# The largest expert's chunks in three parts of two weight tiles, spread over the whole-weight chunks

## The chip, the cores and the metric

The kernel runs on one core of one Trainium2 chip. The metric is the device time of one execution in microseconds (us). Before the change the median of three runs is 2092.88 us (2088.6 to 2093.2). The engines are named as the profile names them: PE (matrix multiply) with PEld (its weight loads), DVE (vector), ACT (scalar), POOL, and SP, which here only issues transfers.

## The reference

The model has two layers. Layer 0 is a mixer and a dense feed-forward network; layer 1 is a mixer and a mixture of experts (MoE). The change is in the MoE alone:

```
logits = (h @ router); top_v, top_i = top_k(logits, 2); gates = softmax(top_v)
for e in range(8):
    out += dense_gate[..., e] * ((silu(h @ w1[e]) * (h @ w3[e])) @ w2[e])
```

There are 256 tokens, `D_MODEL` = 1024 and `D_FF_EXPERT` = 3584. The weights of the eight experts, 3 x 1024 x 3584 float32 values each, are 352 MB, and every one is read once.

## The kernel before

**Experts.** After routing, the experts are put in an order `p`: `p` = 0 is expert 0, and the seven others follow by falling number of tokens. `CAPS` gives each a number of slots: 128, 192, 128, and 64 for each of the five from `p` = 3 on. So `p` = 1 is the largest expert; its 192 tokens lie in two blocks, `xs[1]` (128) and `xs[8]` (64). Tokens are gathered into slots by small matmuls (`gather_k`, L1543) and added back to their rows by others (`comb` in `finish`, L1801). These small pieces are put in a list `fills`, and `fill()` (L1667) runs one of them after each weight tile of `stage_a`.

**Chunks and weight tiles.** The 3584 hidden columns of an expert are handled in 7 chunks of 512. A chunk has six weight tiles of 128 x 2048 float32 (1 MB each): two of w1, two of w3 and two of w2. `stage_a` (L1681) multiplies tokens by the w1 and w3 tiles and forms silu x product; `stage_t` (L1730) transposes this on PE; `stage_b`, called by `stage_2` (L1845), multiplies it by the two w2 tiles. The order is skewed: within `stage_a` of a chunk (after its second tile) the transposes of the chunk before run, and behind `stage_a` comes `stage_2` of the chunk before.

**Whole and split weights.** For `p` >= 3 (`WH` = 3) a tile is used as it lies ("whole"): a float32 matmul with 64 token columns, which takes half of the array, so that two run side by side. For `p` = 0, 1, 2 each tile is split into a high and a low part by `split` (L268): ACT writes the high part from the raw tile (L269), then DVE the low part (L270), and PE multiplies high x high, low x high and high x low in its faster fp32r form (only two products for `xs[8]`, whose high and low tokens lie side by side).

**Order of the chunks.** `jobs` (L1447) holds the seven chunks of `p` = 0, then of 2, then the 35 whole chunks of `p` = 3 to 7. Behind the whole chunks number 2, 7, 12, 17, 22, 27 and 31 it holds one chunk of `p` = 1, as a job like the others. So four split tiles of `p` = 1 come in a row, then four tiles of the next whole chunk, then two more split tiles of `p` = 1.

**Buffers and lookahead.** All weight tiles, raw, high and low alike, come from one pool `w` of `NWT` = 11 buffers (L1406). `plan` lists the loads in the order of use. `prime` (L1426) first sees to it that `LEADS` (5 in this stretch) tiles are in `loaded`, which means that their DMA is issued on SP, and then moves one from `loaded` to `ready`: a whole tile as it is, a split tile by its two instructions, which need two more buffers. `next_w` (L1433) primes until two tiles are in `ready`, and hands out the first. SP issues in order: a load whose buffer isn't free yet holds up the loads behind it. ACT, DVE and PE work in order too; a scheduler of the framework fixes each engine's order when the kernel is built, with the order of the program as its priority.

**Other pools.** Token blocks lie in `xg` (4 buffers of 8 KB per partition), chunk results in `g`, transposed results in `gh` (2 buffers) and `gl`. PSUM banks for chunk results are taken in turn from tags `ax` and `pt`, two banks each.

Of the kernel before, what the change touches and what calls it, by code (L numbers as in the profile page):

```python
# [18 lines left out]
P = 128  # L19
# [148 lines left out]
def tile_backbone(ctx: ExitStack, tc: tile.TileContext, A, out, upto=99, dbg=None):  # L168
# [1278 lines left out]
    jobs = []  # L1447
    job = 0
    for p in (0, 2, 3, 4, 5, 6, 7):
        for c in range(7):  # L1450
            jobs.append((p, c))
            if p >= WH:
                if job in (1, 6, 11, 16, 21, 26, 30):
                    jobs.append((1, sum(j[0] == 1 for j in jobs)))
                job += 1
    ws = {}

    def w_get(p):
        if p not in ws:
            ws[p] = w_of(p)  # L1460
        return ws[p]

    for n in range(len(jobs) + 1):
        if n < len(jobs):
            for i in range(4):
                plan.append(lambda p=jobs[n][0], c=jobs[n][1], i=i: load2(w_get(p)[0](c, i), p >= WH))
        if n:
            for q in range(2):
                plan.append(lambda p=jobs[n - 1][0], c=jobs[n - 1][1], q=q, n=n: load2(w_get(p)[1](c, q), p >= WH,
                                                                                 2 if n == len(jobs) else 1))  # L1470

    def moe(mp, dw, oh0):
# [35 lines left out]
        def xg128():  # L1508
            return Pair(mp.tile([P, 2, KD, P], F32R, tag="xg", name="xg", bufs=4))
# [157 lines left out]
        def fill():  # L1667
            if fills:
                fills.pop(0)()
# [43 lines left out]
        def stage_t0(gd, g3):  # L1713
# [8 lines left out]
            gf = mp.tile([P, 512], F32, tag="gh", name="gf", bufs=2)  # L1722
# [3 lines left out]
            gh, gl_ = [mp.tile([P, 4, P], F32R, tag=n, name=n, bufs=2) for n in ("gh", "gl")]  # L1726
# [3 lines left out]
        def stage_t(gl):  # L1730
# [3 lines left out]
            for g, kind in gl:  # L1734
# [4 lines left out]
                if kind == 0:  # L1739
                    gf = mp.tile([P, 4, 64], F32, tag="gh", name="gf", bufs=2)  # L1740
# [3 lines left out]
                gh = mp.tile([P, 4, P], F32R, tag="gh", name="gh", bufs=2)  # L1744
# [34 lines left out]
        def closing(k):  # L1779
            if k == 0:  # L1780
                end["ss"] = bank("po")
            if not k and "x" not in end:
                end["sq"], end["x"] = [mp.tile([P, KD, 256], F32, tag="xg", name=n, bufs=4) for n in ("sq", "xf")]
                end["dg"] = hp([P, 4, P], "dg")
# [44 lines left out]
        def prep_b():  # L1829
            xs[2], xs[3] = xg128(), [mp.tile([P, KD, 64], F32, tag="xg", name="xf", bufs=4)]  # L1830
            ohTs[2], ohTs[3] = prep([spec(2), spec(3, io=iotd)], [xs[2], xs[3]], True)

        def prep_c(a):
            t = mp.tile([P, 2, KD, 64], F32, tag="xg", name="xf", bufs=4)
            xs[a], xs[a + 1] = [t[:, 0]], [t[:, 1]]
            ohTs[a], ohTs[a + 1] = prep([spec(a, io=iotd), spec(a + 1, io=iotd)], [xs[a], xs[a + 1]], True)
# [27 lines left out]

        prev = None
        gT = []
        for p, c in jobs:
# [14 lines left out]
            gl = stage_a1(*a0) if prev is None else stage_a([xs[1], xs[8]] if p == 1 else [xs[p]], mid)  # L1882
# [98 lines left out]
```

## Time and profile before

| | before |
|---|---|
| median of 3 runs | 2092.88 us |
| profiled execution, own time | 2092.78 us |
| its span (first to last instruction) | 2091.0 us |
| mean granted TensorE clock | 0.984 of full speed |
| busy: PE, PEld, DVE, ACT, POOL | 96%, 66%, 57%, 40%, 5% |
| HBM read | 493.4 MB, mean 236 GB/s over the span |
| weight tiles of the MoE, DMAs of 1 MB | 334 whole, and 2 more in halves |

The profiled execution is the median run to 0.1 us. The span is divided by the page into 40 slices of 52 us; PEclk is the clock granted to PE, DMA the mean busy share of the 16 DMA engines, GB/s what they moved. The MoE's weights move from about 1140 us on; the whole chunks, and with them all chunks of `p` = 1, begin at about 1400 us. A view by stretches gives, for each, the busy time of each engine, the granted clock, the DMA share and the rate. PE's busy time is overstated where matmuls overlap: an instruction of 0.39 us can follow the one before by 0.23 us. So work on PE is counted from start to start.

### The profile page before, as it was taken

To read this page: it belongs to the slowest core of one execution; us is meant where nothing else is said; L and a number is where in the kernel's file an instruction comes from. 1 tells how busy PE (TensorE), PEld (TensorE's weight loads), DVE (VectorE), ACT (ScalarE), POOL (GpSimd) and SP (SyncE) were. 2 spreads that over 40 slices of the span, in tenths; PEclk is the share of its full clock that TensorE was granted. 3 is DMA by queue.
4 is the path that set the end of the run, shared out by engine and by line. 5 is a ranking of instruction groups with operands and counts; after the bars stand their busy time and mean duration, and the time that the engine had idled before them with its cause. 6 is when DMAs were issued, how large, how long until landed. Compare 5 with 4: busy or idle time off the path is not lost. (4 is left out here: it accounts for less than half of the span.)

```text
span 2091.0 us, 26240 instructions
## 1 busy us (share of the span) xinstructions
PE 1999.0 (96%) x10002; PEld 1375.9 (66%) x10002; DVE 1200.4 (57%) x1842; ACT 833.3 (40%) x1261; POOL 109.9 (5%) x148
## 2 busy tenths in 40 slices
PE   7999999889999999999999999998999999899997
PEld 4776756688777878888888888855353544444453
DVE  5366557777566664765477888853253343333443
ACT  4346525643222223544356776733132222222221
POOL 0000015600000000100101000000000000000000
PEclk9999999999999999999999999999999999999998
DMA  8423432025444673322253999996999999899994
GB/s 323 149 91 97 150 121 95 27 65 161 142 150 151 211 237 127 125 61 81 82 230 134 332 364 329 319 375 246 419 368 420 392 419 397 350 398 405 396 382 171
DMA packets 89443, 496.22 MB, mean 237 GB/s; under 512 B 10080, under 2 KB 10848, under 8 KB 46048
## 3 DMA queue, kind: packets, MB, share of 16 engines
q1 hardware_dynamic: 89312, 494.49, 63.7%
q8 instruction: 81, 1.33, 0.3%
q14 instruction: 50, 0.41, 0.1%
HBM read 493.40 MB, written 1.05 MB: 236 GB/s over the span
## 5 line engine op out<-in xcount | busy, mean ns | idle before, releaser
L270 DVE TENSOR_TENSOR w<-w 128x2048 fp32r<-128x2048 f32 (+1 forms) x144 | 289.1, 2022 | 78.3 <-ACT w L269 65.8
L269 ACT ACTIVATE whi<-raw 128x1024 fp32r<-128x1024 f32 x151 | 160.0, 1060 | 406.0 <-PE bk_mm L298 264.8
L269 ACT ACTIVATE w<-w 128x2048 fp32r<-128x2048 f32 (+1 forms) x144 | 241.3, 1699 | 71.2 <-DVE w L270 23.1
L270 DVE TENSOR_TENSOR wlo<-raw,whi 128x1024 fp32r<-128x1024 f32 x151 | 186.1, 1233 | 141.5 <-ACT whi L269 139.1
L297 PE MATMUL bk_mm<-fH,whi 128*128 128x512 f32 (+1 forms) x360 | 139.9, 390 | 2.0 <-DVE xT L518 1.2
L299 PE MATMUL bk_mm<-fH,wlo 128*128 128x512 f32 (+1 forms) x360 | 138.9, 387 | 2.1 <-DVE wlo L270 2.1
L1551 PE MATMUL bk_pt<-w,xf 128*64 128x512 f32 x560 | 138.8, 600 | 1.1 <-ACT g L1704 0.6
L297 PE MATMUL bk_mm<-hH,whi 128*128 128x512 f32 (+1 forms) x384 | 137.4, 361 | 2.3 <-ACT hH L269 2.3
L298 PE MATMUL bk_mm<-fL,whi 128*128 128x512 f32 (+1 forms) x360 | 139.2, 388 | 0.0
L298 PE MATMUL bk_mm<-hL,whi 128*128 128x512 f32 (+1 forms) x384 | 136.2, 356 | 0.0
L299 PE MATMUL bk_mm<-hH,wlo 128*128 128x512 f32 (+1 forms) x384 | 135.5, 354 | 0.0
L1763 PE MATMUL bk_mm<-w,gf 128*64 128x512 f32 x560 | 132.5, 598 | 2.2 <-DMA w<-in_m 1.9
L1551 PE MATMUL bk_ax<-w,xf 128*64 128x512 f32 x560 | 132.7, 596 | 0.1
L1704 ACT COPY g<-bk_ax 64x512 f32<-64x512 f32 x42 | 24.5, 582 | 259.5 <-PE bk_ax L1551 259.3
L456 POOL TENSOR_TENSOR rstd<-rstd,mhalf 128x2 f32<-128x2 f32 (+2 forms) x11 | 10.3, 938 | 1493.3 <-DVE rstd L455 1474.2
L1551 PEld LDWEIGHTS bk_ax<-w,xf 128*64 128x64 f32 x560 | 39.2, 137 | 74.7 <-issue 69.7
L1705 DVE TENSOR_TENSOR g<-g,bk_ax 64x512 f32<-64x512 f32 x42 | 28.4, 675 | 101.3 <-ACT g L1704 101.3
L297 PEld LDWEIGHTS bk_mm<-hH,whi 128*128 128x128 f32 x384 | 71.7, 188 | 21.8 <-issue 5.4
L1763 PEld LDWEIGHTS bk_mm<-w,gf 128*64 128x64 f32 x560 | 38.1, 136 | 71.3 <-issue 68.4
L1551 PEld LDWEIGHTS bk_pt<-w,xf 128*64 128x64 f32 x560 | 38.7, 136 | 69.2 <-issue 63.4
L297 PEld LDWEIGHTS bk_mm<-fH,whi 128*128 128x128 f32 x360 | 68.1, 190 | 22.6 <-issue 3.6
L298 PEld LDWEIGHTS bk_mm<-hL,whi 128*128 128x128 f32 x384 | 72.2, 188 | 13.2 <-issue 3.4
(568 smaller groups left out, 4364.3 us busy)
## 6 DMA issues: line engine op xcount, KB each, us to landing
w<-in_m SPq DMA_DIRECT2D x334, 1024.0 KB, 9.5
raw<-in_f SPq DMA_DIRECT2D x66, 512.0 KB, 3.7
araw<-in_adc SPq DMA_DIRECT2D x56, 512.0 KB, 4.0
araw<-in_ada SPq DMA_DIRECT2D x32, 512.0 KB, 7.0
raw<-in_evx SPq DMA_DIRECT2D x29, 512.0 KB, 3.7
raw<-in_odx SPq DMA_DIRECT2D x22, 512.0 KB, 3.6
raw<-in_evo SPq DMA_DIRECT2D x12, 512.0 KB, 3.7
xT<-in_xt SPq DMA_DIRECT2D x4, 1024.0 KB, 5.5
```

The costliest lines, as they stand in the source:

```text
L269: a = S.activation(hi, src, AF.Copy)
L270: v = V.tensor_tensor(lo, src, hi.bitcast(F32), op=ALU.subtract)
L297: T.matmul(o, wh, xh, start=first, stop=False)
L298: T.matmul(o, wh, xl, start=False, stop=False)
L299: T.matmul(o, wl, xh, start=False, stop=last)
L456: G.tensor_tensor(r, r, mhalf[:, :n], op=ALU.pow)
L1551: T.matmul(o[c:c + 64], sl(b[0]), wh, start=k < 2, stop=k >= K - 2, tile_position=(0, c))
L1704: S.copy(g[0:64], hb[b][0][64:128])
L1705: V.tensor_tensor(g[0:64], g[0:64], hb[b][0][0:64], op=ALU.add)
L1763: T.matmul(accs[0][half][64 * q2:64 * q2 + 64], gT[0][0][:, f, :], wh[:, hs], start=first and q == 0, stop=last and q == 1, tile_position= ...
```

## The change

The order of work becomes a list `seq` of whole-chunk entries `(p, c, None)` and of parts `(1, c, part)`. A chunk of `p` = 1 is three parts of two split tiles each: part 0 the w1 tiles, part 1 the w3 tiles, part 2 the w2 tiles. The 21 parts are spread by the count of whole chunks; at most one stands between two whole chunks. By the formula they stand behind whole chunks 3, 5, 6, 8, 9, 11, 12, 14, 15 and so on to 32 and 33: two parts for every three whole chunks.

```diff
-    for p in (0, 2, 3, 4, 5, 6, 7):
-        for c in range(7):
-            jobs.append((p, c))
-            if p >= WH:
-                if job in (1, 6, 11, 16, 21, 26, 30):
-                    jobs.append((1, sum(j[0] == 1 for j in jobs)))
-                job += 1
+    for p in (0, 2, 3, 4, 5, 6, 7):
+        for c in range(7):
+            seq.append((p, c, None))
+            if p >= WH:
+                whole_chunks += 1
+                while parts < min(21, (whole_chunks - 1) * 21 // 32):
+                    seq.append((1, parts // 3, parts % 3))
+                    parts += 1
```

The lookahead counts `loaded` and `ready` together (six tiles), and whole tiles may be handed on ahead, up to four in `ready`, until a split tile stands in `ready`. So the two instructions of a split come up to three tiles earlier in the program:

```diff
-        while plan and len(loaded) < n:
+        while plan and (not loaded or len(loaded) + max(len(ready), 1) < n + 1):
             fetch()
...
-        while len(ready) <= AHEAD and (loaded or plan):
+        while (len(ready) <= AHEAD or len(ready) < 4 and all(w[1] is None for w in ready)) and (loaded or plan):
             prime()
```

A new function `unit` does a part. Its instructions are those that `stage_a` and `stage_2` did for `p` = 1; the result of part 0 waits in two tiles of a new tag `gb` (2 buffers) for part 1. The transposes for part 2 are done within the whole chunk ahead of it, behind that chunk's own.

```diff
+        def unit(c, part):
+            if part == 2:
+                stage_2(1, c, gTb.pop())
+                return
+            blocks = [xs[1], xs[8]]
+            hb = [bank("ax") for _ in blocks]
+            for q in range(2):
+                wh, wl = next_w()
+                for k4 in range(4):
+                    k, cs = q * 4 + k4, slice(k4 * 512, k4 * 512 + 512)
+                    for o, blk in zip(hb, blocks):
+                        mmb(o, blk, lambda x: x[:, k, :], wh[:, cs], wl[:, cs], k == 0, k == 7, k, 8)
+                fill()
...
             def mid():
-                if prev is not None:
-                    gT.append(stage_t(prev[1]))
+                gT.append(stage_t(prev[1]))
+                if n + 1 < len(seq) and seq[n + 1][2] == 2:
+                    gTb.append(stage_t(list(zip(big, (2, 1)))))
```

Besides, `xg` has 3 buffers in place of 4 (the blocks of `p` = 3 to 6 share one of them), and `gh` has 3 in place of 2.

## Rows read from the trace of the kernel before

**Rows 1.** The page's view of the span in 40 equal slices: the rate of all transfers.

```profile
GB/s 323 149 91 97 150 121 95 27 65 161 142 150 151 211 237 127 125 61 81 82 230 134 332 364 329 319 375 246 419 368 420 392 419 397 350 398 405 396 382 171
```

**Rows 2.** The view by stretches for the whole stage of the whole chunks. Columns: from:to, length, busy us (and instructions) of PE, PEld, DVE, ACT, POOL, granted clock, DMA share, GB/s.

```profile
1400.00:2060.00 660.00, 621.76 (x2756) 308.96 (x2754) 251.45 (x312) 173.22 (x211) 0.00 (x0) 0.97 0.94 382
```

**Rows 3.** The same view, the stage cut so that stretches with splits of `p` = 1 and stretches without alternate.

```profile
1400.00:1470.00 70.00, 63.98 (x274) 38.34 (x272) 28.61 (x32) 21.45 (x33) 0.00 (x0) 0.93 0.72 283
1470.00:1510.00 40.00, 38.38 (x186) 12.89 (x184) 9.65 (x16) 7.18 (x12) 0.00 (x0) 1.00 1.01 420
1510.00:1560.00 50.00, 45.69 (x198) 28.52 (x195) 24.59 (x27) 17.70 (x17) 0.00 (x0) 0.97 0.91 367
1560.00:1610.00 50.00, 47.11 (x224) 16.64 (x222) 12.67 (x21) 8.25 (x13) 0.00 (x0) 1.00 1.01 418
1610.00:1660.00 50.00, 47.02 (x192) 29.17 (x192) 21.98 (x19) 15.36 (x15) 0.00 (x0) 0.93 0.96 390
1660.00:1700.00 40.00, 38.71 (x188) 13.82 (x186) 13.13 (x24) 7.40 (x13) 0.00 (x0) 1.00 1.01 419
1700.00:1750.00 50.00, 48.33 (x210) 28.62 (x208) 23.33 (x22) 17.60 (x17) 0.00 (x0) 1.00 0.98 395
1750.00:1800.00 50.00, 45.71 (x217) 15.36 (x214) 12.65 (x22) 10.35 (x15) 0.00 (x0) 1.00 1.01 421
1800.00:1850.00 50.00, 44.67 (x182) 28.88 (x181) 21.95 (x22) 14.53 (x14) 0.00 (x0) 0.90 0.82 323
1850.00:1900.00 50.00, 46.41 (x221) 16.05 (x219) 13.33 (x22) 9.42 (x14) 0.00 (x0) 1.00 1.01 420
1900.00:1950.00 50.00, 47.42 (x195) 29.53 (x194) 21.24 (x19) 14.41 (x15) 0.00 (x0) 0.93 0.94 380
1950.00:1980.00 30.00, 30.00 (x147) 10.82 (x144) 11.20 (x21) 7.11 (x12) 0.00 (x0) 1.00 1.01 421
1980.00:2060.00 80.00, 78.33 (x350) 40.32 (x346) 37.11 (x50) 22.46 (x26) 0.00 (x0) 1.00 0.95 381
```

**Rows 4.** The same view for single places: a stretch of `p` = 0 and 2 (every tile split), the stop at the first chunk of `p` = 1, a place of two-tile splits, a place of four-tile splits, and the end of the loads.

```profile
1200.00:1250.00 50.00, 50.00 (x222) 40.31 (x221) 42.75 (x24) 34.84 (x24) 0.00 (x0) 1.00 0.99 365
...
1410.00:1430.00 20.00, 14.50 (x58) 11.13 (x58) 7.30 (x5) 9.81 (x18) 0.00 (x0) 0.74 0.17 59
...
1550.00:1560.00 10.00, 10.00 (x46) 7.07 (x45) 7.43 (x9) 2.40 (x2) 0.00 (x0) 1.00 0.67 248
...
1700.00:1730.00 30.00, 29.32 (x130) 18.21 (x128) 13.50 (x11) 11.21 (x10) 0.00 (x0) 1.00 1.01 419
...
2050.00:2060.00 10.00, 10.00 (x51) 3.60 (x50) 3.02 (x6) 0.90 (x2) 0.00 (x0) 1.00 0.81 312
2060.00:2070.00 10.00, 9.51 (x47) 3.24 (x48) 2.80 (x5) 1.47 (x3) 0.00 (x0) 1.00 0.01 2
```

**Rows 5.** Groups of instructions from 1400 to 2060 us: line, engine, operation, tiles, shapes and count, then busy us, mean ns of one, and idle time before them with what ended it.

```profile
L1763 PE MATMUL bk_mm<-w,gf 128*64 128x512 f32 x528 | 125.2, 598 | 2.2 <-DMA w<-in_m 1.9
L270 DVE TENSOR_TENSOR w<-w 128x2048 fp32r<-128x2048 f32 x42 | 95.9, 2290 | 55.3 <-ACT w L269 51.7 <-DMA w<-in_m 3.1
L269 ACT ACTIVATE w<-w 128x2048 fp32r<-128x2048 f32 x42 | 80.3, 1911 | 48.7 <-PE bk_ax L1559 23.1 <-DMA w<-in_m 20.1 <-DVE w L270 5.4
L1554 PE MATMUL bk_ax<-w,xg 128*128 128x512 f32 x56 | 25.8, 461 | 9.5 <-ACT w L269 9.5
L1555 PE MATMUL bk_ax<-w,xg 128*128 128x512 f32 x56 | 25.8, 460 | 7.3 <-DVE w L270 7.3
...
L1555 PE MATMUL bk_ax<-w,gh 128*128 128x512 f32 x28 | 11.7, 418 | 5.4 <-DVE w L270 5.4
```

**Rows 6.** PE in order of time: start, us, line, operation, tiles, count. First the combination of one result block (four matmuls, L1815 and L1816) up to the next matmul, then the 40 matmuls of the two w3 tiles of `p` = 1 up to the next whole tile, then one whole chunk from its first matmul to that of the next one.

```profile
1400.83 0.39 PE L1815 MATMUL bk_ada<-ohT,yh 128*128 128x256 f32 x1
...
1401.50 1.94 PE L1551 MATMUL bk_pt<-w,xf 128*64 128x512 f32 x8
...
1433.72 0.39 PE L1554 MATMUL bk_pt<-w,xg 128*128 128x512 f32 x1
...
1443.18 3.65 PE L1763 MATMUL bk_mm<-w,gf 128*64 128x512 f32 x16
...
1466.55 3.65 PE L1551 MATMUL bk_ax<-w,xf 128*64 128x512 f32 x16
...
1477.45 3.60 PE L1551 MATMUL bk_ax<-w,xf 128*64 128x512 f32 x16
```

**Rows 7.** The first stop. SP's longest wait between 1410 and 1430 us, then ACT in order of time at the end of the stop (evacuations of gathers, L1536, and the first split, L269), then the first matmul of `p` = 1 on PE.

```profile
SPq L1412 <- DVE w L270: 12.8, 1, 12.8
```

```profile
1419.01 0.31 ACT L1536 ACTIVATE xf<-bk_ada,mod 128x64 f32<-128x64 f32 x1 [1.31 <-PE bk_ada L1526]
1419.22 1.90 ACT L269 ACTIVATE w<-w 128x2048 fp32r<-128x2048 f32 x1
```

```profile
1421.17 0.80 PE L1554 MATMUL bk_ax<-w,xg 128*128 128x512 f32 x1 [2.20 <-ACT w L269]
```

**Rows 8.** Weight tiles issued between 1380 and 1410 us: number, size, median us from issue to landing.

```profile
w<-in_m SPq DMA_DIRECT2D x9, 1024.0 KB, 8.8
```

**Rows 9.** PE at the end: the last weight matmuls, and the first matmul of the last combination.

```profile
2066.17 5.37 PE L1763 MATMUL bk_mm<-w,gf 128*64 128x512 f32 x24
2071.53 0.38 PE L1815 MATMUL bk_ax<-ohT,yh 128*128 128x256 f32 x1
```

More of the change, by code (lines that the diff above doesn't have):

```diff
@@ L1461, in w_get, with plan_tiles @@
         return ws[p]
[L1463 to L1470, printed above, removed]
+    def plan_tiles(p, c, ins, outs, parts=1):
+        for i in ins:
+            plan.append(lambda p=p, c=c, i=i: load2(w_get(p)[0](c, i), p >= WH))
+        for q in outs:
+            plan.append(lambda p=p, c=c, q=q: load2(w_get(p)[1](c, q), p >= WH, parts))
+    last = None
+    for p, c, part in seq:
+        if part is None:
+            plan_tiles(p, c, range(4), ())
+            if last:
+                plan_tiles(*last, (), range(2))
+            last = p, c
+        elif part < 2:
+            plan_tiles(p, c, range(2 * part, 2 * part + 2), ())
+        else:
+            plan_tiles(p, c, (), range(2))
+    plan_tiles(*last, (), range(2), 2)
     def moe(mp, dw, oh0):
@@ L1743, in stage_t @@
                     continue
-                gh = mp.tile([P, 4, P], F32R, tag="gh", name="gh", bufs=2)
+                gh = mp.tile([P, 4, P], F32R, tag="gh", name="gh", bufs=3)
                 if kind == 2:
@@ L1782, in closing @@
             if not k and "x" not in end:
-                end["sq"], end["x"] = [mp.tile([P, KD, 256], F32, tag="xg", name=n, bufs=4) for n in ("sq", "xf")]
+                end["sq"], end["x"] = [mp.tile([P, KD, 256], F32, tag="xg", name=n, bufs=3) for n in ("sq", "xf")]
                 end["dg"] = hp([P, 4, P], "dg")
@@ L1829, in prep_b @@
         def prep_b():
-            xs[2], xs[3] = xg128(), [mp.tile([P, KD, 64], F32, tag="xg", name="xf", bufs=4)]
+            xs[2], t = xg128(), mp.tile([P, 4, KD, 64], F32, tag="xg", name="xf", bufs=3)
+            for i in range(4):
+                xs[3 + i] = [t[:, i]]
             ohTs[2], ohTs[3] = prep([spec(2), spec(3, io=iotd)], [xs[2], xs[3]], True)
         def prep_c(a):
-            t = mp.tile([P, 2, KD, 64], F32, tag="xg", name="xf", bufs=4)
-            xs[a], xs[a + 1] = [t[:, 0]], [t[:, 1]]
+            if a == 6:
+                xs[7] = [mp.tile([P, KD, 64], F32, tag="xg", name="xf", bufs=3)]
             ohTs[a], ohTs[a + 1] = prep([spec(a, io=iotd), spec(a + 1, io=iotd)], [xs[a], xs[a + 1]], True)
@@ L1863, in stage_2 @@
                 finish(ysp[1], 8, ohTs[8])
+        big, gTb = [], []
+        def unit(c, part):
[11 more added lines that the diff above has]
+                fill()
+            if part == 0:
+                big[:] = [mp.tile([P, 512], F32, tag="gb", name="gb", bufs=2) for _ in blocks]
+                S.activation(big[0], hb[0], AF.Silu)
+                g = big[1][0:64]
+                S.copy(g, hb[1][64:128])
+                V.tensor_tensor(g, g, hb[1][0:64], op=ALU.add)
+                S.activation(g, g, AF.Silu)
+                return
+            V.tensor_tensor(big[0], big[0], hb[0], op=ALU.mult)
+            g, g3 = big[1][0:64], mp.tile([64, 512], F32, tag="g", name="g3", bufs=3)
+            S.copy(g3, hb[1][64:128])
+            V.tensor_tensor(g3, g3, hb[1][0:64], op=ALU.add)
+            V.tensor_tensor(g, g, g3, op=ALU.mult)
         prev = None
         gT = []
-        for p, c in jobs:
+        for n, (p, c, part) in enumerate(seq):
+            if part is not None:
+                unit(c, part)
+                continue
             if (p, c) == (0, 1):
```

14 lines of the change are left out of this document (7 added, 7 removed).

## The prediction

> **What bounds the kernel now.** I read the rate by slices first [rows 1]: only from about the twenty-third slice on does the rate go to 320 GB/s and above. That is the MoE. All that the change touches lies between 1400 us, where the whole chunks begin, and the end, so I read that stage alone. It moved 0.382 x 660 = 252.1 MB in 660 us [rows 2].
>
> Next, the stage in stretches [rows 3]. The reader is to see two kinds that alternate. Where no tile is split, the DMA share is 1.01 and the rate 418 to 421 GB/s: the transfers set the pace and PE follows. Where tiles of `p` = 1 are split, the rate falls to 283, 367, 390, 395, 323, 380, 381. Against 420 GB/s this is time lost, length x (1 - rate/420): 22.8 + 6.3 + 3.6 + 3.0 + 11.5 + 4.8 + 7.4 = 59.4 us. About 2 us of the last lie behind the last landing, since the slice from 2050 has a share of 0.81 and the next 0.01 [rows 4]; so loads end at about 2058 us and the loss is 57.4 us. 22.8 us of it is at the first chunk of `p` = 1, and 34.6 us at the six others.
>
> Why it is lost: at the first chunk the DMA share is 0.17 for 20 us [rows 4]. SP waits 12.8 us for one buffer, which DVE frees by a split [rows 7]; that split stands in ACT's and DVE's order behind evacuations of gathers, and PE's first matmul of `p` = 1 waits for it until 1421 us. So PE, SP and ACT hold each other up: a row of four split tiles takes eight buffers beyond its four raw ones, of 11 in all.
>
> PE is the other limit. A whole chunk takes 1477.45 - 1466.55 = 10.9 us and two split tiles 1443.18 - 1433.72 = 9.46 us [rows 6]. From 1400 to 2060 us there are 528/16 = 33 whole chunks [rows 5], 21 pairs of split tiles and 28 combinations (four each for `p` = 2 to 6, eight for `p` = 1) at 0.67 us [rows 6]: 360 + 199 + 19 = 578 us of 660. A tile of 1.049 MB at 420 GB/s lands each 2.50 us, so a whole chunk is 15.0 us of transfers against 10.9 us of PE, and a pair of split tiles 5.0 against 9.46. Neither engine is the bound throughout; what is lost is lost because the two kinds of work come in lumps that 11 buffers can't level.
>
> **The change part by part.** Instructions: the same 1 MB loads, the same 42 splits in this stage at 1.91 us on ACT and 2.29 us on DVE [rows 5], the same matmuls, transposes, evacuations. Nothing is removed or added, only moved; the static cost is 0. The narrower pools: `xg` with 3 buffers still has each block's buffer free when it is gathered (the block of `p` = 7 takes that of `p` = 2, done before), so I cost them at nothing; were it not so, PE would wait once for one chunk, 11 us at most.
>
> The order. Two parts for three whole chunks are 18 + 4 = 22 tiles, 54.9 us of transfers, against 3 x 10.9 + 2 x 9.46 = 51.6 us of PE, and about 1.6 us for combinations (24 over 31 whole chunks). So each period is nearly level, and transfers lead by a little. How far PE falls behind within a period: a part adds 9.46 - 5.0 = 4.5 us, a whole chunk takes off 4.1. Part, whole, part gives 4.5 - 4.1 + 4.5 = 4.9 us, and the next two whole chunks take off 8.2. Before: four split tiles 8.9, minus 4.1, plus 4.5: 9.3 us. Where a split is not begun ahead, its 1.91 + 2.29 = 4.2 us come on top in both. So the lag at the worst place is about half. In buffers: (4.9 + 4.2)/2.50 = 3.6 tiles landed and not used, one in use, three for pairs, leave 3.4 of 11 for loads under way. At full rate a load took 8.8 us to land [rows 8], 8.8/2.50 = 3.5 under way. It just fits.
>
> What is left of the loss, term by term.
> - The first stop, 22.8 us: from 0 to 22.8. The first part comes one whole chunk later, with two split tiles in place of four, and four of the eight gathers done by then. I take 3.
> - The 20 other parts. Bound below 0: between 1700 and 1730 us a group of four split tiles ran at 419 GB/s [rows 4]. Bound above: 34.6 us over six chunks is 12 groups, 2.9 us for a group, if a group costs the same whatever its size; by tiles it is 34.6/36 = 0.96 us, 1.9 for a part. As the lag is half, I take half of 1.9, 0.95 us: 19 us for 20 parts.
> - The end. The last weight matmuls end at 2071.5 us [rows 9], 13.5 behind the last landing. In the new order the last group leaves 4.4 us less lag, but two whole chunks follow it in place of three (4.1 less taken off): 0, between -8 and +5.
>
> Sum: 57.4 - 3 - 19 = 35.4 us. From the profiled execution's own 2092.8 us, which is the median of the three runs to 0.1 us: **2057 us**.
>
> Does PE fit into that? Up to the new end of its weight matmuls, 2071.5 - 35.4 = 2036, it has 636 us for 578 + 10 (what it did from 2060 to 2071) + about 10 for transposes of `p` = 1: 38 us are left for waits and low clock. Its waits for splits were 9.5 + 7.3 + 5.4 = 22.2 us [rows 5]; and a granted clock of 0.93, 0.97, 0.93, 0.90, 0.93 in the mean (it goes between 2.4 and 1.2 GHz) cost it 4.9 + 1.5 + 3.5 + 5.0 + 3.5 = 18 us more [rows 3], always where it had stood still. This is close: a part may expose no more than 38/21 = 1.8 us. The cover is the early split; without it, see the second rival.
>
> Two rules speak to whether the loss can be had back at all. The whole stretches show 418 to 421 GB/s [rows 3]. The Trainium skill, page "DMA: Bandwidth & Descriptors", Specifications, gives an HBM limit of about 358 GB/s for a core; by that the 252.1 MB would take 704 us, more than they did, and no order could gain; by the rows it is 600 us, so the rows decide.
>
> The second: in rows 3 the shares alone leave 19.6 + 4.5 + 2 + 1 + 9 + 3 + 4 - 2 = 41 us idle, and 16 us of the loss is a low rate under busy DMA engines, as in 1200 to 1250 us (0.99 and 365 GB/s with DVE busy 43 of 50 us) but not in 1700 to 1730 (419, DVE 13.5 of 30) [rows 4]. If splits slow transfers, those 16 us stay, since the number of splits stays, and 41 us is the most to be gained (2052 us). The Trainium skill, page "SBUF — State Buffer", Who interferes with whom, says a DMA never contends with a compute engine; by that all 57 us could be had (2035 us). My 22 us left over lie beyond both.
>
> **The rivals.**
> - *Loss goes by tiles, not by lag.* Each part costs 1.9 us and the first 5: 57.4 - 38.6 - 5 = 14 us, 2079 us. For it: two-tile groups lost as well as four-tile ones (4.1 us in 1550 to 1560 us, 10 x (1 - 248/420)) [rows 4]. Against: there the lag of the four before them was still there.
> - *PE becomes the bound.* If each of 21 parts exposes what a group of four did, 22.2/7 = 3.2 us, because raw tiles land just when they are wanted and an early place in the order helps nothing, PE needs 598 + 67 = 665 us from 1400: 2065 in place of 2071.5, 2086 us; with the 18 us of low clock as before, 2104. The middle, 2095 us, is no change. For it: transfers lead by only 1.7 us a period, so PE often stands before a split. Against: standing still is then paid by a lag that hides the next split.
> - *Slower: pairs that stand early take the buffers.* A split begun three tiles ahead turns one buffer into two for 7.5 us, 21 times; SP, in order, then waits for a buffer at each part. It decides from 57.4/21 = 2.7 us for a part; at the 4.1 us of the place above it is 86 us, 28.7 more than before: 2121 us. For it: the count above leaves 3.4 buffers where 3.5 are wanted. Against: the total of `loaded` and `ready` is held at six.
>
> **How the numbers follow.** Chances: forecast, 2040 to 2070 us, 0.47; still better, down to both floors (all 57 us and some of the end, 2030), 0.08; by tiles, 2070 to 2086, 0.20; PE bound, 0.12; slower by buffers, 0.13. A measurement of this kernel can tell about 0.3%, 6.3 us, from no change. Faster: 0.47 + 0.08 + 0.20 = 0.75. Same: most of the PE case, 0.10. Slower: the rest of it and the last, 0.15. The range from 2034 to 2093 us leaves out half of the best case, the upper half of the PE case and the slower one, about 0.2; the likeliest case's own range is 2040 to 2070 us.
>
> **What would show it.** Right: the shares of the stretches all near 1.0 with no stop of 10 us or more; the rate from 1400 us to the last landing near 405 GB/s (252 MB in some 622 us); the last landing near 2022 us and the end the same 35 us behind it. Rates near 390 mean loss by tiles. Shares below 0.9 with PE never idle mean PE is the bound; shares below 0.9 with SP waiting for DVE splits or for `p` = 1 matmuls, the buffers. A time above 2087 us would make the forecast wrong, and a first stop that stays would take 20 us from it.

## The result and the profile after: 21 us slower

The changed kernel takes 2114.02 us (median of 4 runs, 2113.66 to 2116.38) against 2093.04 us for the kernel before on the same chip: ratio 1.0099, 95% interval 1.0084 to 1.0114. The prediction was 2057 us, with slower at 0.15. It was wrong in sign and size.

The profiled execution took 2114.17 us, its span is 2112.4 us, and the first matmul of the whole chunks starts at 1367.55 us, before at 1369.65. So all of the loss lies in the stage that the prediction was about. First the page's rate in 40 slices:

```profile
GB/s 322 152 88 101 150 123 81 31 61 179 138 152 139 238 241 85 129 61 82 139 160 219 341 357 319 319 395 324 375 316 388 387 364 397 394 380 396 325 389 161
```

Up to the twenty-sixth slice the same work runs as before [rows 1]; the slices are 1% longer and cut it at other places. Behind it, slices of 410 to 420 (before: 419, 420, 419) are gone; the best is 397. The view by stretches of the stage shows the same (columns as in rows 2):

```profile
1400.00:2080.00 680.00, 637.61 (x2735) 304.00 (x2736) 245.05 (x306) 168.96 (x210) 0.00 (x0) 0.98 0.93 370
...
1400.00:1470.00 70.00, 63.04 (x270) 27.87 (x270) 19.21 (x28) 18.95 (x33) 0.00 (x0) 0.95 0.83 333
1470.00:1520.00 50.00, 48.22 (x206) 24.53 (x204) 17.77 (x20) 8.74 (x12) 0.00 (x0) 0.97 0.93 372
1520.00:1570.00 50.00, 42.67 (x173) 21.91 (x170) 19.56 (x24) 13.99 (x15) 0.00 (x0) 0.93 0.82 325
1570.00:1620.00 50.00, 47.90 (x215) 21.82 (x215) 16.03 (x21) 10.93 (x15) 0.00 (x0) 1.00 0.97 383
1620.00:1670.00 50.00, 49.00 (x212) 22.44 (x209) 15.66 (x16) 12.07 (x13) 0.00 (x0) 1.00 1.00 410
1670.00:1720.00 50.00, 44.40 (x200) 21.81 (x199) 21.45 (x32) 13.48 (x18) 0.00 (x0) 0.97 0.90 353
...
1770.00:1820.00 50.00, 47.59 (x212) 23.67 (x210) 18.01 (x19) 13.61 (x15) 0.00 (x0) 1.00 1.00 397
...
1870.00:1920.00 50.00, 49.33 (x219) 22.77 (x218) 14.53 (x18) 12.84 (x16) 0.00 (x0) 1.00 0.99 404
1920.00:1970.00 50.00, 44.80 (x186) 22.10 (x185) 18.63 (x25) 11.52 (x14) 0.00 (x0) 0.93 0.91 366
1970.00:2020.00 50.00, 47.44 (x204) 22.76 (x204) 16.33 (x19) 10.23 (x13) 0.00 (x0) 0.97 0.90 353
...
1420.00:1440.00 20.00, 15.66 (x62) 8.72 (x63) 6.28 (x5) 6.78 (x13) 0.00 (x0) 0.83 0.49 178
1430.00:1440.00 10.00, 6.49 (x18) 4.58 (x18) 4.49 (x2) 4.12 (x4) 0.00 (x0) 0.66 0.61 210
...
2070.00:2080.00 10.00, 10.00 (x49) 3.80 (x46) 3.81 (x9) 1.74 (x3) 0.00 (x0) 1.00 0.78 296
2080.00:2090.00 10.00, 9.63 (x48) 3.80 (x48) 5.10 (x11) 1.37 (x3) 0.00 (x0) 1.00 0.00 1
```

The reader is to see three things. The last landing is near 2077.8 us (a share of 0.78 in the slice from 2070, 0.00 in the next); before it was near 2058 [rows 4]. The bytes are the same, 0.370 x 680 = 252 MB, so against 420 GB/s the loss is 677.8 - 251.6/0.42 = 79 us, where it was 57.4. That is 21.6 us more, the whole slowdown: 2092.8 + 21.6 = 2114.4. And the loss is now spread over the whole stage: the three best stretches reach 397, 404 and 410 GB/s, and the others lose 4 us or more in 50, where before stretches of 418 to 421 alternated with poor ones [rows 3]. The stretch with the first stop, 1400 to 1470 us, loses 70 x (1 - 333/420) = 14.5 us, where it lost 22.8; the stop itself is the two slices of 178 GB/s and the one behind them. The other twenty parts lose 79 - 14.5 = 64.5 us, 3.2 us each.

Splits and their matmuls from 1400 to 2080 us, as groups (columns as in rows 5):

```profile
L270 DVE TENSOR_TENSOR w<-w 128x2048 fp32r<-128x2048 f32 x42 | 94.7, 2283 | 6.7 <-ACT w L269 6.7
L269 ACT ACTIVATE w<-w 128x2048 fp32r<-128x2048 f32 x42 | 77.9, 1903 | 0.0
L1566 PE MATMUL bk_ax<-w,xg 128*128 128x512 f32 x112 | 48.8, 436 | 11.7 <-DVE w L270 11.7
L1565 PE MATMUL bk_ax<-w,xg 128*128 128x512 f32 x112 | 48.8, 435 | 2.4 <-ACT w L269 2.4
```

The durations are those of rows 5. What changed is the idle time before the splits: ACT waited 48.7 us before them, now 0.0. A split on ACT no longer waits for data or for a buffer; it stands in ACT's order behind an evacuation, and PE waits for it. What the waits of SP and PE in that stretch say (us in total, times, longest):

```profile
SPq L1412 <- PE bk_pt L1570: 190.9, 39, 8.9
SPq L1412 <- PE bk_ax L1562: 126.8, 54, 8.4
...
PE bk_ax L1566 <- DVE w L270: 24.7, 22, 2.3
...
PE bk_ax L1565 <- ACT w L269: 3.7, 2, 2.4
```

PE waits for the low part 22 times, about once a part, up to 2.3 us. Together with the high part that is 28.4 us, where it was 22.2 [rows 5]: 6 us more, of a slowdown of 21. SP's largest wait is for the last matmuls of `p` = 1 on a split tile (L1570): a load stands behind a buffer that such a tile still holds. In the kernel before, SP's waits for the same matmuls (L1559) came to 76.7 + 70.8 = 147.5 us. One place in order of time (start, us, engine, line, operation) shows the link:

```profile
1740.72 0.58 ACT L1718 COPY g<-bk_pt 64x512 f32<-64x512 f32 x1 [0.60 <-PE bk_pt L1562]
...
1741.20 3.71 ACT L269 ACTIVATE w<-w 128x2048 fp32r<-128x2048 f32 x2
...
1744.05 0.46 PE L1749 MATMUL bk_po<-ca,g 64*128 64x64 f32 x4
...
1744.43 0.51 PE L1565 MATMUL bk_ax<-w,xg 128*128 128x512 f32 x1
...
1744.54 0.42 DVE L1752 COPY gf<-bk_po 128x256 f32<-128x256 f32 x1 [1.81 <-PE bk_po L1749]
...
1744.88 4.48 DVE L270 TENSOR_TENSOR w<-w 128x2048 fp32r<-128x2048 f32 x2
...
1747.22 0.50 PE L1566 MATMUL bk_ax<-w,xg 128*128 128x512 f32 x1 [2.05 <-DVE w L270]
```

The lookahead has issued the split up to three tiles early in the program, but the built order puts it right behind the last evacuation of the whole chunk ahead of the part (L1718) on ACT, and behind the copy of that chunk's transposes (L1752) on DVE. That copy can run only when PE has done the transposes (L1749), and then PE stands directly before the part. So of 1.90 + 2.28 us a whole DVE instruction is still to come when PE arrives. This happens mostly at a group's first tile; before a second tile PE stood twice, 2.2 us each.

PE's own time shows where the rest of the slowdown is. The stage from 1400 us to the end of the last weight matmul, first before the change, then after it (columns as in rows 2):

```profile
1400.00:2071.50 671.50, 632.77 (x2806) 312.48 (x2804) 254.25 (x317) 175.38 (x214) 0.00 (x0) 0.97 0.92 376
```

```profile
1400.00:2093.70 693.70, 650.79 (x2798) 308.86 (x2798) 250.24 (x316) 170.98 (x213) 0.00 (x0) 0.98 0.91 363
```

PE is busy for all but 38.7 us before and 42.9 us after. For a tile to land it waits 2.4 us before and at no place after. So of 22.2 us more only 4.2 are idle time; for 18.0 us PE is busy longer, with the same matmuls. One reason stands in its built order. Here the second tile of the part above is begun, left for matmuls of the next whole chunk, and taken up again:

```profile
1751.31 0.39 PE L1570 MATMUL bk_pt<-w,xs1b 128*128 128x512 f32 x1
1751.63 3.65 PE L1562 MATMUL bk_ax<-w,xf 128*64 128x512 f32 x14
1755.21 0.51 PE L1565 MATMUL bk_ax<-w,xg 128*128 128x512 f32 x1
1755.55 0.40 PE L1569 MATMUL bk_pt<-w,xs1b 128*128 128x512 f32 x1
1755.88 0.64 PE L1562 MATMUL bk_ax<-w,xf 128*64 128x512 f32 x1
...
1757.74 0.50 PE L1566 MATMUL bk_ax<-w,xg 128*128 128x512 f32 x1
1758.08 0.39 PE L1567 MATMUL bk_ax<-w,xg 128*128 128x512 f32 x1
```

A matmul of `p` = 1 follows the one before by 0.23 us, but by 0.34 behind such a switch, and a whole one follows by 0.32. In the row of 14 whole matmuls twelve run in pairs and the last two one by one, so that it takes 3.58 us, as long as 16 in pairs (3.53 us in the kernel before, from 1477.45). Counted in PE's timeline, its order switches between whole matmuls and those of `p` = 1 28 times before the change (two for each group) and 98 times after it; 38 whole matmuls run alone before and 70 after. At about 0.17 us for a switch and 0.21 for a matmul alone, both read at this place, that is an estimate of 70 x 0.17 + 32 x 0.21 = 19 us, of 18.0 to explain.

### The profile page after: what moved, and what is told of

Its sections match the earlier page's. It is cut to its first block, busy times and chain, and to the rows that moved or that the text cites. A ratio compares the mean times of both kernels' runs of the same rounds, so it can differ in the third digit from the quotient of the medians.

```text
span 2112.4 us, 26200 instructions
## 1 busy us (share of the span) xinstructions
PE 2017.1 (95%) x10002; PEld 1370.6 (65%) x10002; DVE 1196.7 (57%) x1842; ACT 829.3 (39%) x1261; POOL 110.0 (5%) x148
## 5 line engine op out<-in xcount | busy, mean ns | idle before, releaser
L269 ACT ACTIVATE whi<-raw 128x1024 fp32r<-128x1024 f32 x151 | 159.9, 1060 | 407.3 <-PE bk_mm L298 265.5
L269 ACT ACTIVATE w<-w 128x2048 fp32r<-128x2048 f32 (+1 forms) x144 | 239.0, 1697 | 22.5 <-DVE w L270 17.7
L1562 PE MATMUL bk_ax<-w,xf 128*64 128x512 f32 x560 | 147.6, 601 | 0.0
L1562 PE MATMUL bk_pt<-w,xf 128*64 128x512 f32 x560 | 147.5, 600 | 0.0
L1774 PE MATMUL bk_mm<-w,gf 128*64 128x512 f32 x560 | 144.9, 596 | 0.5 <-DVE gf L1752 0.5
L1566 PE MATMUL bk_ax<-w,xg 128*128 128x512 f32 x224 | 93.8, 419 | 12.4 <-DVE w L270 12.4
L1565 PE MATMUL bk_ax<-w,xg 128*128 128x512 f32 x224 | 93.3, 417 | 2.4 <-ACT w L269 2.4
L1567 PE MATMUL bk_ax<-w,xg 128*128 128x512 f32 x224 | 90.6, 405 | 0.0
L1774 PEld LDWEIGHTS bk_mm<-w,gf 128*64 128x64 f32 x560 | 42.6, 137 | 70.1 <-issue 67.5
```

The source lines that it names most:

```text
L269: a = S.activation(hi, src, AF.Copy)
L1562: T.matmul(o[c:c + 64], sl(b[0]), wh, start=k < 2, stop=k >= K - 2, tile_position=(0, c))
L1565: T.matmul(o, sl(b[0]), wh, start=first, stop=False)
L1566: T.matmul(o, sl(b[0]), wl, start=False, stop=False)
L1567: T.matmul(o, sl(b[1]), wh, start=False, stop=last)
L1774: T.matmul(accs[0][half][64 * q2:64 * q2 + 64], gT[0][0][:, f, :], wh[:, hs], start=first and q == 0, stop=last and q == 1, tile_position= ...
```

## The experiments

Fifteen kernels ran, each beside the kernel before, whose median lay between 2091.6 and 2092.8 us there; the ratios are to that. "Loss" is that of the stage, computed as above from each profile: last landing less 1400 us, less the bytes at 420 GB/s. "PE" is its busy and its idle time from 1400 us to the last weight matmul, from each profile. A group is a run of split tiles between two whole chunks.

| kernel | groups | median us | ratio to before, 95% | loss, us | PE busy + idle, us |
|---|---|---|---|---|---|
| before | 14 | 2093.0 | | 57 | 633 + 39 |
| after | 21 | 2114.0 | 1.0084 to 1.0114 | 79 | 651 + 43 |
| spread_late | 21 | 2098.3 | 1.002 to 1.004 | 61 | 643 + 34 |
| lumps_early | 14 | 2086.6 | 0.9955 to 0.9982 | 52 | 633 + 32 |
| spread_forced | 21 | 2115.1 | 1.0073 to 1.0131 | 77 | 659 + 32 |
| spread_ahead3 | 21 | 2102.2 | 1.0025 to 1.0059 | 65 | 647 + 33 |
| lumps_units | 14 | 2089.0 | 0.9969 to 0.9990 | 53 | 630 + 38 |
| groups14 | 14 | 2094.6 | 0.9999 to 1.0023 | 59 | 631 + 47 |
| spread_pieces | 21 | 2074.3 | 0.9889 to 0.9941 | 37 | 623 + 27 |
| spread_first_pieces | 21 | 2089.2 | 0.9974 to 0.9998 | 53 | 643 + 25 |
| spread_second_pieces | 21 | 2119.8 | 1.0122 to 1.0156 | 80 | 655 + 44 |
| lumps_pieces | 14 | 2074.3 | 0.9906 to 0.9939 | 40 | 628 + 26 |
| spread_late_pieces | 21 | 2071.8 | 0.9893 to 0.9926 | 33 | 624 + 24 |
| lumps_early_pieces | 14 | 2061.8 | 0.9840 to 0.9873 | 28 | 619 + 22 |
| groups14_pieces | 14 | 2069.5 | 0.9864 to 0.9913 | 30 | 612 + 27 |
| spread_10 | 21 | 2146.4 | 1.0242 to 1.0281 | | |
| spread_late_10 | 21 | 2128.5 | 1.0162 to 1.0202 | | |

The theories: *group* (the loss goes by the number of groups, because PE arrives before each group's first split is done), *tiles* (it goes by split tiles, whose number is unchanged), *buffers* (pairs begun early hold buffers that loads want).

### The two halves of the change, one at a time

`spread_late`: the new order with the old lookahead. `lumps_early`: the old order with the new lookahead.

```diff
 # spread_late, from after
-        while plan and (not loaded or len(loaded) + max(len(ready), 1) < n + 1):
+        while plan and len(loaded) < n:
...
-        while (len(ready) <= AHEAD or len(ready) < 4 and all(w[1] is None for w in ready)) and (loaded or plan):
+        while len(ready) <= AHEAD and (loaded or plan):
 # lumps_early, from before: the same lines the other way
```

> The spread order with the lookahead of before (one edit undone: splits are not begun ahead). Buffers theory (pairs that are begun early hold buffers that SP's next loads need): faster than the changed kernel's 2114 us, towards 2095. Group theory (each group of split tiles exposes its first split, because ACT and DVE hold that split behind the evacuations of the whole chunk ahead; 21 groups in place of 14, at about 3 us each): within 4 us of 2114, since the order on ACT is nearly the same with and without the early place in the program.

> The order of before (lumps of four and two split tiles) with the new lookahead alone. Buffers theory: slower than before's 2093 us, by some 14/21 of the 21 us, 2105 to 2110. Group theory: 14 groups as before, 2093 within 4 us.

The new order alone costs about 6 us, the early lookahead 16 us on top of it; in the old order the same lookahead gains 5 to 6 us. So neither half has a price of its own: the lookahead's sign depends on the order. The group theory failed at the first run (within 4 us of 2114 was expected, 2098.3 came) and the buffers theory had it; at the second run it was the other way, 2105 to 2110 expected by buffers and 2086.6 measured, better than either said. SP's three largest waits in `spread_late`:

```profile
SPq L1412 <- PE bk_pt L1562: 138.6, 43, 6.7
SPq L1412 <- PE bk_mm L1774: 138.1, 43, 10.2
SPq L1412 <- PE bk_pt L1570: 119.0, 42, 3.8
```

Against after, the wait for `p` = 1's matmuls (L1570) is 119.0 in place of 190.9 us and at most 3.8 in place of 8.9. PE's waits for splits are 21.2 us, less than the 28.4 with the early lookahead.

### Is it the place of the split in the engines' order, or the code?

`spread_forced`: a whole chunk's evacuations are ordered behind a split that has been begun ahead. `lumps_units`: the changed code with the parts at the old places.

```diff
 # spread_forced, from after (begun: the two instructions of the last split)
+                    with ExitStack() as st:
+                        if ready and ready[-1][1] is not None:
+                            for ins in begun:
+                                st.enter_context(tc.issue_after(ins))
+                        S.copy(g[0:64], hb[b][0][64:128])
...
 # lumps_units, from after
-                while parts < min(21, (whole_chunks - 1) * 21 // 32):
+                n1 = whole_chunks in (2, 7, 12, 17, 22, 27, 31) and 2 or whole_chunks in (3, 8, 13, 18, 23, 28, 32) and 1 or 0
+                for _ in range(n1):
```

> The changed kernel, with the evacuations of a whole chunk (ACT and DVE) ordered behind the split that was begun ahead, so that the split's place in the engines' order is early too. Group theory: PE's waits for splits, 28 us from 1400 us on in the changed kernel, fall below 10 us and the time falls by 10 to 30 us, to 2085 to 2104. Buffers theory: the pair stands still earlier and longer, so 2114 us or more.

> The new code (parts, early lookahead, narrower pools) with the parts at the places of the old order: parts 0 and 1 together, part 2 behind the next whole chunk. If the order alone makes the change slower: as the old code with the early lookahead, 2083 to 2090 us. If the new code or its narrower pools cost: nearer to 2114 us.

Forcing the place gained nothing, as the buffers theory had said: PE's waits for splits fell only from 28.4 to 21.5 us (the group theory wanted under 10), and ACT then waited 43.3 us for the raw tiles to land. An early place does not help a tile that isn't there yet. PE's idle time did fall, from 43 to 32 us, but its busy time rose by 8: in the order that was built 122 whole matmuls run alone, after the change 70. `lumps_units` at 2089.0 us clears the code and the narrower pools: with them and the old places the loss is 53 us, as in `lumps_early`. What is slower is the order, with this lookahead.

### Splits in four pieces

The kernel has a switch (`NSPC`) that cuts the first few splits into pieces of 512 columns; here it cuts all of them, so that PE's first matmuls need only the first piece. `spread_first_pieces` and `spread_second_pieces` cut only the first or the second split of each part of `p` = 1.

```diff
 # spread_pieces, lumps_pieces, spread_late_pieces, lumps_early_pieces, groups14_pieces
-    NSPC = 4
+    NSPC = 999
 # spread_first_pieces, from after (== 0 for spread_second_pieces); 84 splits come before p = 1
+        nsplit[0] += 1
+        if nsplit[0] > 84 and nsplit[0] % 2 == 1:
+            cols = 512
         for i in range(0, 2048, cols):
```

> The changed kernel, with each split done in four pieces of 512 columns, so that PE can begin on a tile after a quarter of its split. Group theory: the exposed part falls from about 4 us to under 2 for a group, 15 to 30 us faster than 2114. Buffers theory: nothing changes in which buffers are held, 2114 us within 5.

> After with only the first of the two splits of each part in four pieces; all others whole. Group theory (what costs is that PE stands before the first split of a group, 1.9 us on ACT and 2.3 us on DVE for each of 21 groups): nearly all of the 40 us that pieces gave, 2074 to 2082 us. Tile theory (each split costs by itself): half, about 2094 us. If pieces gave their gain through the splits of the other two split experts or by letting evacuations pass between pieces anywhere: 2094 us or above.

> After with only the second of the two splits of each part in four pieces. Group theory: the second split lies under the matmuls of the first tile (4.7 us for a tile against 4.2 us for a split), so nothing, 2108 to 2116 us. Tile theory: half, about 2094 us.

With all splits cut, the new order goes from 2114.0 to 2074.3 us, 40 us, and all of it lies in this stage. Its view by stretches, PE's wait for splits, and a part's start (from the view by stretches, the waits and the timeline of `spread_pieces`):

```profile
1400.00:2035.00 635.00, 608.71 (x2719) 294.33 (x2718) 252.68 (x428) 180.53 (x335) 0.00 (x0) 1.00 0.98 395
1420.00:1430.00 10.00, 9.17 (x45) 4.53 (x42) 4.19 (x7) 5.10 (x13) 0.00 (x0) 1.00 0.31 107
```

```profile
PE bk_ax L1566 <- DVE w L270: 5.6, 13, 0.9
```

```profile
1748.39 4.27 ACT L269 ACTIVATE w<-w 128x512 fp32r<-128x512 f32 x8
...
1752.30 0.50 PE L1565 MATMUL bk_ax<-w,gh 128*128 128x512 f32 x1
...
1752.41 0.42 DVE L1752 COPY gf<-bk_po 128x256 f32<-128x256 f32 x1 [2.49 <-PE bk_mm L1774]
1752.76 4.90 DVE L270 TENSOR_TENSOR w<-w 128x512 fp32r<-128x512 f32 x8
...
1753.49 0.50 PE L1566 MATMUL bk_ax<-w,gh 128*128 128x512 f32 x1 [0.24 <-DVE w L270]
```

The place is of the same kind as the one in after: DVE again comes to the split only behind L1752, at the moment at which PE stands there. But PE waits 0.24 in place of 2.05 us, since one piece is enough. The granted clock is 1.00 over the whole stage, where after had stretches of 0.93 to 0.97 and a slice of 0.66, and the DMA share is 0.98 in place of 0.93.

The halves tell which split it is. Cutting the first one alone gains 25 us of the 40, the second alone none (5.8 us slower, which no theory said; by the profiles 1.4 us of that lie in this stage). The group theory expected nearly all from the first. With it cut, PE's waits for splits are these in `spread_first_pieces` (its L1570 is L1566 of after):

```profile
PE bk_ax L1570 <- DVE w L270: 8.4, 13, 2.2
...
PE bk_ax L1569 <- ACT w L269: 1.1, 1, 1.1
```

28.4 us have become 9.5, and 5.6 with both cut. So the last 15 us need both (`spread_pieces` also cuts the splits ahead of the stage), but they aren't a wait for the second split: PE stands before a second tile twice, 2.2 us each, as in after, and its idle time is 25 us with the first cut and 27 with all. What falls is its busy time, from 643 to 623 us: the order that was built for `spread_pieces` has 70 switches in place of 98, and 26 whole matmuls alone in place of 83.

> The kernel before with every split in four pieces of 512 columns. If the 40 us that pieces gave in the new order came from the first split of each group being waited for by PE, 14 groups gain 40 x 14/21 = 27 us: about 2066 us. If pieces only help where pairs are begun early and hold buffers (buffers theory), nothing: 2088 to 2093 us. If the order alone is better once splits are cheap to wait for, this one is slower than the new order with pieces (2074 us).

> The new order with the old lookahead and splits in pieces. Buffers theory: the early lookahead costs its 16 us by the buffers that pairs hold, and that is apart from the wait for a split, so both gains add up: 2074 - 16 = 2058 us. Group theory alone (the lookahead costs only because PE waits longer and holds the buffers meanwhile): with pieces the lookahead no longer matters, 2070 to 2078 us.

> The old order with the new lookahead and splits in pieces. If gains add up: the lookahead gave 5 us in the old order, pieces 27 by the group theory: 2093 - 32 = 2061 us. If the new order is in itself the better one once splits are cheap, not below 2074 us. Buffers theory: four tiles in a row begun early hold eight buffers, so slower than the old order with the old lookahead and pieces.

Pieces gain 18 us in the old order (27 expected by the group theory). With the late lookahead the two orders are then alike, 2074.3 and 2071.8 us: all that the new order gives, once splits are cheap to wait for, is not to be told from no change. In the new order the early lookahead, which cost 16 us with splits in one piece, costs 2.5 us with pieces, less than the 7 us over which the four runs of `spread_pieces` spread; the buffers theory's 2058 us fell. In the old order pieces and early lookahead gain 30 us together, more than the 18 + 5 of each alone: 2061.8 us, the best kernel of the study, 1.3 to 1.6% faster than before. Its stage to the last landing, and the slice with the landing:

```profile
1400.00:2030.00 630.00, 608.83 (x2750) 301.38 (x2748) 257.58 (x436) 184.14 (x336) 0.00 (x0) 0.99 0.97 400
...
2020.00:2030.00 10.00, 9.50 (x48) 3.54 (x48) 2.76 (x6) 1.16 (x2) 0.00 (x0) 1.00 0.76 292
```

### The number of groups

`groups14`: the changed code with the parts evenly spread in 14 groups, parts 0 and 1 together and part 2 alone. `groups14_pieces`: the same with splits in pieces.

```diff
-                while parts < min(21, (whole_chunks - 1) * 21 // 32):
-                    seq.append((1, parts // 3, parts % 3))
-                    parts += 1
+                while parts < 21 and groups < (whole_chunks - 1) * 14 // 32:
+                    for _ in range(1 if parts % 3 else 2):
+                        seq.append((1, parts // 3, parts % 3))
+                        parts += 1
+                    groups += 1
```

> After's code with 14 groups spread evenly (parts 0 and 1 together, part 2 alone) in place of 21 groups of two tiles. Group theory (loss is 2.9 to 3.8 us for a group, whatever its size; after lost 79 us over 21): 14 groups lose 14 x 3.7 = 52 us, 27 less than after, so about 2087 us. Tile theory (loss goes by the 42 split tiles): as after, 2114 us. Buffers theory (pairs begun early hold buffers; a row of four tiles holds more): 2114 us or more.

> 14 evenly spaced groups, early lookahead, splits in pieces. With pieces the new order (21 groups) gave 2074 us and the old one (14 groups) with the same lookahead 2062 us. If what is left of the difference is the number of groups: about 2062 us or a little less, since the groups stand evenly. If it is the old code or its wider pools: about 2074 us.

Same code, same lookahead, same 42 split tiles: 14 groups in place of 21 take 19.4 us off, of 27 expected by the group theory. The tile theory is out. With the early lookahead and splits in one piece the loss for a group is 79/21 = 3.8, 77/21 = 3.7, 52/14 = 3.7, 53/14 = 3.8 and 59/14 = 4.2 us, whether a group has two tiles or four. With the late lookahead it doesn't go by groups: 57 us before with 14, 61 in `spread_late` with 21, and with pieces 40 with 14 and 33 with 21. `groups14_pieces` lies 4.8 us under `spread_pieces`, but its four runs spread from 2061.7 to 2073.0 us and its profile is that of the fastest, so with pieces the early lookahead's 37/21 = 1.8, 28/14 = 2.0 and 30/14 = 2.1 settle little.

Nor is the price of a group PE's standing before its first split. PE waits 27.8 us for splits in `groups14` and 28.4 in after, and its idle time is even 4 us longer; what is shorter is its busy time, 631 us in place of 651, at 30 switches and 33 whole matmuls alone in place of 98 and 70. `spread_late` has 70 switches and 90 alone, 643 us busy. This is read from the traces; no run changed PE's order and nothing else.

### The early lookahead and the buffers

`spread_10` and `spread_late_10`: 10 weight buffers in place of 11. `spread_ahead3`: three tiles handed on ahead in place of four.

```diff
-    AHEAD, LEAD, NWT, PRE, SPL = 1, 4, 11, (1, 3, 5, 7), (1, 3)
+    AHEAD, LEAD, NWT, PRE, SPL = 1, 4, 10, (1, 3, 5, 7), (1, 3)
 # spread_ahead3
-        while (len(ready) <= AHEAD or len(ready) < 4 and all(w[1] is None for w in ready)) and (loaded or plan):
+        while (len(ready) <= AHEAD or len(ready) < 3 and all(w[1] is None for w in ready)) and (loaded or plan):
```

> After with 10 weight buffers in place of 11. Buffers theory (the early lookahead cost 16 us in the new order since pairs stand in buffers that loads want): one buffer less costs clearly more here than with the late lookahead, 2130 us or above. If the buffers are not what binds: within 6 us of after, 2108 to 2120 us.

> The new order with the late lookahead (2098 us with 11 buffers) and 10 weight buffers. Buffers theory: the late lookahead has about one buffer to spare, so it loses less than the early one does, and with 10 buffers it is near what the early one was with 11: 2105 to 2115 us. If buffers do not bind: 2094 to 2102 us.

> After with the limit of tiles handed on ahead at three in place of four, so that a split is begun up to two tiles early (late lookahead, one tile: 2098 us; after, three: 2114 us). If the early lookahead costs in proportion to the time that a pair stands in two buffers: half way, 2104 to 2108 us. If it costs by one wait that appears only when the pair is allocated ahead of a certain load (order of the loads on SP): at one of the two ends, 2098 or 2114 us.

By their times the first two look like a verdict for the buffers: 32 and 30 us for one buffer (the second is above both ranges). The trace says otherwise. The first whole chunk on PE, in `spread_10`:

```profile
1393.53 1.07 PE L1562 MATMUL bk_ax<-w,xf 128*64 128x512 f32 x2
```

In after that matmul starts at 1367.55 us, in `spread_late` at 1368.71, in `spread_late_10` at 1396.83. The profiled spans are 33.8 and 31.5 us longer; 26.0 and 28.1 us of that were lost before the stage, where every tile is split. In the stage itself a buffer less costs 7.8 us with the early lookahead and 3.4 with the late one: more with the early one, as the buffers theory said, but not the 16 us and more that it wanted. So a plain shortage of buffers is unlikely to be the whole of the 16 us; more than 11 buffers were not tried.

`spread_ahead3` lies between, 2102.2 us, 2 us under the range for half way: 4 us for the first tile further ahead, 12 for the second. With SP's wait for L1570 (119.0, 144.5 and 190.9 us for one, two and three tiles ahead) this fits a load that comes to stand behind a buffer of a pair which PE frees later and later. But that wait is no measure of the loss: it is 137.0 us in `spread_second_pieces` (there L1574), which loses 80 us, and 147.5 in before, which loses 57. By PE's time the 16 us are about 8 us of idle time, nearly all before splits, and 8 us of busy time (643 + 34 against 651 + 43). Why the early lookahead gives this order these two is open; no run took either away by itself.

## Why the prediction was wrong

**What bounds the kernel.** The loss against 420 GB/s did follow the time (the span ends 34.6 us behind the last landing, 32.9 before; forecast 35). But that neither engine is the bound, and that where no tile is split "the transfers set the pace and PE follows", doesn't hold. Rows 6 show a whole chunk at PE's own pace, 10.9 us, in such a stretch, where the transfers' pace would be 15.0: PE works off tiles that have landed. It waits 2.4 us for loads in the stage before and none after. Its time, busy and idle, is the whole stage; where DMA engines idle, loads wait for a buffer.

**The failed step: "As the lag is half, I take half of 1.9, 0.95 us: 19 us for 20 parts".** Measured: 64.5 us, 3.2 us a part. The bullet held the better figure as its upper bound, "2.9 us for a group, if a group costs the same whatever its size". With it, 20 x 2.9 + 14.5 = 72.5 us are left, 15 more than before: 2108 us. I took the loss to be lag, which grows with a group's length and can be halved by cutting groups in two. It didn't halve with either lookahead: the finer order went from 57 to 61 us with the late one and from 52 to 79 with the early one. With the early one it goes by groups, 3.7 to 4.2 us each.

**"Nothing is removed or added, only moved; the static cost is 0."** This fell with it. With the same matmuls PE's busy time grew by 18.0 us and its idle time by 4.2; the switches in its built order and the whole matmuls that run alone account for about 19 us, an estimate. Had I counted PE's time before the change, 632.8 us busy and 38.7 idle of 671.5, I would have seen that it was full: my 598 us of work, 22.2 of waits and 18 of low clock are 638 us, 33 short.

**The first stop, 3 us.** Measured 14.5 in the stretch that lost 22.8. It shrank, as the mechanism said, but by a third; the size was off by 11.5 us. These two terms are the whole error: 45.5 + 11.5 = 57 us, and 2057 + 57 = 2114.

**"The cover is the early split."** The step fell. I priced the early place in the program as an early place on the engines. The built order put the split behind L1718 and L1752, and rows 5 had a warning in it: before the change ACT waited 48.7 us ahead of its splits, so the splits were already waiting for data and buffers more than for their turn. Without the early split, in `spread_late`, ACT waits 0.0 us ahead of splits too and PE less for them, 21.2 us in place of 28.4. PE's exposure, 1.35 us a part, stayed under the 1.8 that the forecast allowed, and the time was missed all the same.

**The slots, "It just fits".** At 3.4 to 7.8 us for one buffer less in this stage, the count alone wasn't what decided.

**The rivals.** *By tiles* fell with `groups14`. *PE becomes the bound* had the right engine and the wrong term: PE's time sets the end, after the change and before it, but its waits for splits are 28.4/21 = 1.35 us a part and not 3.2, and most of what was added is busy time. *Slower by buffers* came nearest in the number, 2121 us, with SP behind the matmuls of `p` = 1 as it said; but the order alone was already slower with the late lookahead, and with pieces, which hold the same buffers, the early lookahead costs 2.5 us, within the spread of the runs. What the runs show: the new order costs about 6 us with the late lookahead and 27 with the early one (2086.6 against 2114.0), 19 of which go when the parts stand in 14 groups. That the larger part of it is PE's busy time is read from the traces and was not tried by itself.

**The two rules.** The HBM limit that I set aside stays aside. On whether splits slow transfers: `spread_pieces` has a share of 0.98 from 1400 to 2035 us and 395 GB/s, where at 420 for a share of 1.01 it would be 408. The Trainium skill, page "SBUF — State Buffer", Who interferes with whom, says that a DMA never contends with a compute engine; by that these 13 GB/s must have another cause, and no run isolates it.

A rule that I had not weighed fits what was found. The Trainium skill, page "Perfetto Trace Analysis", Optimizing Scalar/DVE Operations, says that where ACT and DVE aren't saturated but cause bubbles on other engines, breaking up their instructions may let work be completed sooner. In this stage ACT was busy 169 of 680 us and DVE 245, and cutting was worth 40 us. The Trainium skill, page "Perfetto Trace Analysis", Optimization Strategy, says that interleaving regimes with different bounds may improve performance. Here interleaving more finely cost about 6 us with whole splits and gave 2.5, no measurable difference, with pieces, both with the late lookahead; with the early one it cost 27 and 12 us.

## What to carry to other kernels

Before interleaving two kinds of work more finely, ask what each change from one to the other costs by itself, and count the changes in the order that was built for the engine with the least idle time: here the plan had 42 and the built order 98. A loss seen on the DMA side may be time that this engine spends. An instruction issued earlier in the program runs earlier only if its place in each engine's order, and its data, come earlier too; read that from ACT and DVE around the first consumer. Where a consumer waits for a long instruction at a change, cut the producer into pieces first: here this was worth 18 to 40 us, with either order.

## What was unexpected of the hardware

Pieces are cheap. Two tiles take ACT 3.71 us whole and 4.27 in eight pieces, DVE 4.48 and 4.90 (two whole splits at 1744.88 us in after, eight pieces in `spread_pieces`): (4.27 - 3.71)/6 = 0.093 us for each further instruction on ACT, (4.90 - 4.48)/6 = 0.07 on DVE. The Trainium skill, page "Perfetto Trace Analysis", Optimizing Scalar/DVE Operations, gives a data-access overhead for each instruction of about 93 ns for ScalarE and 60 ns for DVE on SBUF; the trace agrees for ACT and is near for DVE.

A wait of PE costs more than itself. From 1430 to 1440 us after has PE busy 6.49 of 10 us at a granted clock of 0.66, so part of that slice ran at 1.2 GHz in place of 2.4. PE had stood there for 2.41 and 1.10 us; behind that its matmuls take 0.63 us and follow each other by 0.43, until they take 0.39 again and follow by 0.23:

```profile
1438.82 0.63 PE L1565 MATMUL bk_ax<-w,xg 128*128 128x512 f32 x1
...
1440.26 0.39 PE L1565 MATMUL bk_ax<-w,xg 128*128 128x512 f32 x1
```

In `spread_pieces`, without such stops, the clock is 1.00 in the stage.

The built order costs PE time of its own. A whole matmul that runs alone takes the 0.43 us of a pair, and the first matmuls behind a switch follow later by about 0.1 us, as the rows from 1751 us show.
